# First mixer of a two-layer decoder trunk: GpSimd's wide elementwise work moved to VectorE

## The chip, the cores and the metric

The kernel runs on one core of a Trainium2 chip. The metric is device time in microseconds, the median over several executions. One more execution was profiled; all rows below come from it. The engines are named as in the profile: PE is TensorE (PEld its weight loads), DVE is VectorE, ACT is ScalarE, POOL is GpSimd, SP is SyncE, which issues the loads.

## What is computed

A trunk of two layers over 256 tokens of width 1024, in float32. Each layer has a token mixer (HGRN2, a gated linear recurrence, in the first layer; native sparse attention in the second) and a gated ConvFFN. Each of these is preceded by an RMS norm whose output is scaled and shifted by rows of a modulation that come from a conditioning vector `c`. The part of the reference that the change touches:

```
c_act = jax.nn.silu(c)
for layer in range(DEPTH):
    mod = c_act @ ada_w[layer] + ada_b[layer]
    sh1, sc1, g1, sh2, sc2, g2 = [m[:, None, :] for m in jnp.split(mod, 6, axis=-1)]
    hmix = rmsnorm(x, norm_mix[layer]) * (1.0 + sc1) + sh1
    ...
    x = x + g1 * y
...
proj = h @ w_in                                   # HGRN2: queries, gates f, values i, output gates g
log_f = jnp.log(lb + (1.0 - lb) * jax.nn.sigmoid(f_pre))
k = (1.0 - lb) * jax.nn.sigmoid(-f_pre)
...
    b = jnp.cumsum(lfc, axis=2)
    o_inter = jnp.einsum('bhtk,bhkv->bhtv', qc * jnp.exp(b), state)
    scores = jnp.einsum('bhtk,bhsk,bhtsk->bhts', qc, kc, decay)
    o_intra = jnp.einsum('bhts,bhsv->bhtv', scores, vc)
```

## The kernel before

Activations are feature-major: eight chunks of 128 features by 256 tokens. Every float32 product is made of three: the operands are split into a high and a low part (`hi`, `lo`), and the products high-high, high-low and low-high are added up in PSUM (`mm3`, L315).

**The stream of weights.** All weights pass in units of 128 x 1024 (512 KB), in the order of their use (`Stream`, L68). SP loads a unit into one of seven buffers `raw` (L93); a load starts when an earlier unit's buffer comes free. A unit of a weight is split: ScalarE rounds it to `whi` (L106) and another engine subtracts, `wlo = raw - whi` (L113). Five pairs of split parts exist. A unit of the modulation (`ada`) has one row of its weight per partition; its product with `silu(c)`, held on all partitions in `cb`, is summed along the columns into one column of `mod`. VectorE does that in one instruction with a sum (L244). GpSimd does the product alone (L241), and ScalarE then copies it with a sum (L242). Sixteen rows belong to the opening, 24 to the rest of the mixer, where they stand among the weights.

**The opening** (to about 75 us, L471). Instructions of VectorE, ScalarE and GpSimd go out here in the order of the code. One step per chunk: a row of the modulation, the chunk's scale and shift (`gs_t`, `sh_t`), the normed chunk `xn`, its high part `XH` on ScalarE and its low part `XL` on VectorE, and the split of the chunk's two units of weights. TensorE multiplies each chunk as soon as it is there. GpSimd has the second row of each of seven steps, and in chunks 2 to 5 (`U1`) half of the second low part.

**The recurrence** (class `HG`, L539, for four heads at a time, group A and then group B). `prepare` makes queries `Q`, decays `T` and keys `KS` out of PSUM, where GpSimd scales the keys (L575). Then `chain`: the scores of the diagonal (L585), five levels (m = 1 to 16; `level`, L592, scores L599) and three larger blocks (`blocks`, L622, scores L630, L641, L648). After each, `grow` multiplies half of the queries `QP` (VectorE, L617) and half of the keys (GpSimd, L618) by `T`, in two instructions of 256 columns each, and the next level's scores need both. Masked copies (L588, L605) take the scores out of PSUM on VectorE. `values` (L657) and `turn` (L689) make the outputs, which `finish_out` projects and adds to the residual (L448).

TensorE and SP follow the order of the code everywhere. While group A's chain runs, TensorE has the products for the queries and gates of group B beside it; beside group B's chain it has those of the output gates. Outside the opening a scheduler orders VectorE, ScalarE and GpSimd by priority; what the chain needs has `soon()`, and splits and rows fill in.

Of the six units ahead of the mixer's later rows GpSimd makes three low parts whole (`HG_LOW`), and of the 24 later rows it has every second one (`HG_POOL`).

Of the kernel before, what the change touches and what calls it, by code (L numbers as in the profile page):

```python
# [21 lines left out]
NC = 8            # feature chunks of D  # L22
S = 256
EPS = 1e-6
H = 8             # HGRN2 heads
LEVELS = (1, 2, 4, 8, 16)
G = 4             # NSA key/value groups
# [3 lines left out]
NJ = 22           # chunks of the ConvFFN's width  # L31
NJ0 = 4           # of them, those of a ConvFFN's first products
BIG = 3.0e38
# Order of issue. Units are 1024 columns of a weight, priorities are instructions.
RAWS, SPLITS = 7, 5           # buffers of loaded and of split units
LOOK = (7, 3)                 # units loaded and split ahead of the one in use
SOON = 90                     # priority of what the tensor engine waits for
QSOON = (150, 150, 25, 25)    # the same for a group's queries
TSOON = 75                    # and for probabilities turned
U1 = range(2, 6)              # opening chunks whose second low part DVE and Pool share  # L40
HG_LATE = 6                   # units ahead of the first units of the modulation, in HGRN2
FFN_LATE = 8                  # and in a ConvFFN
HG_POOL = 2                   # every how many of the former go to Pool
HG_LOW = (0, 1, 2)            # units whose low part goes to Pool
NSA_LOW = (6, 8)
NSA_LOW2 = (0, 2, 5)
NSA_ROWS = (11, 3)            # units of the modulation among the keys' and values', and behind them
NSA_SPLIT = 2                 # units split between the values' products
PRE = 2                       # units loaded ahead across a norm
HG_WEAVE = (16.4, 15.5)       # times of the second chain of HGRN2 and of the products beside it  # L50
HG_TURN = 14                  # of these, steps ahead of the first heads' turn
HG_OUT = (1, 3)               # heads projected in the chain, and up to the second heads' turn
# [15 lines left out]


class Stream:  # L70
    """Weights in the order of their use, in units of 1024 columns: loads run ahead of the splits into two
    float32r parts, and the splits ahead of the products."""

    def __init__(self, nc, raw_pool, split_pool, look_load, look_split):
# [1174 lines left out]
```

## Time and profile before

| | |
|---|---|
| device time, median of 3 runs | 777.64 us (776.15 to 781.36) |
| span of the profiled execution | 774.9 us |
| busy in it: PE, DVE, ACT, POOL | 725.1, 598.5, 410.4, 230.6 us |
| instructions of POOL | 247 |

The profile gives the span of its own execution, first to last instruction; what a run's time has beyond that it does not list. Busy time is the time in which an engine has an instruction open, whether it moves or not. In a timeline row stand the start and the length in us, then engine, line, operation, output<-inputs, size, and in brackets the idle time ahead of it and what ended that. In a row of a group stand its count and busy time, the mean of one in ns, and the idle time ahead.

### The profile page before, as it was taken

The numbers are of one execution on the slowest core, as the hardware profiler recorded it, in microseconds if no ns is written. First come the engines' busy times: TensorE is split into PE (matmuls) and PEld (weight loads), VectorE is DVE, ScalarE is ACT, GpSimd is POOL, SyncE is SP. The second block draws the span as 40 slices with busy tenths as digits, with TensorE's granted clock in tenths as the row PEclk, the third lists the DMA queues.
The fourth block names the chain that finished last, engine by engine and source line by source line (L and its number), as shares of the span: only waits on it lengthen the run. The fifth ranks groups of instructions, "written<-read, shape, count | busy, mean of one in ns | idle before, by whom it ended". The sixth has DMA issues, their size and how long they took to land.

```text
span 774.9 us, 14443 instructions
## 1 busy us (share of the span) xinstructions
PE 725.1 (94%) x5492; PEld 678.1 (88%) x5492; DVE 598.5 (77%) x1041; ACT 410.4 (53%) x756; POOL 230.6 (30%) x247
## 2 busy tenths in 40 slices
PE   7879888888999999999999999999999999999996
PEld 6767778768999999999989987756889999999995
DVE  5999987898599788778969877886768866666653
ACT  4456325426366444446545676776545744555544
POOL 4455647564203135111130015543520201101102
PEclk8999989999999999999999999987999999999998
DMA  8789655755368888899957960010237666776701
GB/s 302 269 274 313 204 191 191 268 192 193 110 219 300 297 280 270 294 267 341 344 191 254 355 207 21 35 56 1 85 134 271 196 217 214 215 221 210 209 18 55
DMA packets 48855, 160.45 MB, mean 207 GB/s; under 512 B 9362, under 2 KB 9618, under 8 KB 48787
## 3 DMA queue, kind: packets, MB, share of 16 engines
q1 hardware_dynamic: 48496, 159.02, 61.8%
q8 instruction: 43, 0.70, 0.4%
q10 hardware_dynamic: 290, 0.53, 0.2%
q14 instruction: 26, 0.20, 0.1%
HBM read 158.48 MB, written 1.05 MB: 206 GB/s over the span
## 4 chain that ended last, share of the span: by engine, by line
PE 72%; DVE 14%; issue 5%; POOL 5%; ACT 3%; DMA 2%; POOLq 0%; DVEq 0%; ACTq 0%
PE mm L316 10%; PE mm L318 10%; PE mm L317 10%; PE acc L379 9%; PE acc L317 7%; PE acc L316 7%; PE acc L318 7%; DVE wlo L113 4%; DVE raw L244 4%; PE acc L1006 2%; PE aux L1076 2%; PE aux L599 2%; POOL wlo L113 1%; PE acc L1005 1%; DMA raw<-ada 1%
## 5 line engine op out<-in xcount | busy, mean ns | idle before, releaser
L113 DVE TENSOR_TENSOR wlo<-raw,whi 128x1024 fp32r<-128x1024 f32 x193 | 247.1, 1291 | 66.8 <-ACT whi L106 66.5
L106 ACT CAST whi<-raw 128x1024 fp32r<-128x1024 f32 x201 | 207.9, 1047 | 138.2 <-PE acc L317 56.3
L316 PE MATMUL mm<-XH,whi 128*128 128x256 f32 x640 | 180.8, 283 | 1.0 <-DVE ff L791 0.9
L318 PE MATMUL mm<-XH,wlo 128*128 128x256 f32 x640 | 178.7, 279 | 0.0
L317 PE MATMUL mm<-XL,whi 128*128 128x256 f32 x640 | 178.4, 279 | 0.0
L796 POOL TENSOR_TENSOR fl<-ff,fh 128x256 fp32r<-128x256 f32 x44 | 43.9, 1002 | 302.9 <-ACT fh L794 297.8
L244 DVE SCALAR_TENSOR_TENSOR raw<-raw,cb 128x1024 f32<-128x1024 f32 x77 | 107.1, 1392 | 25.3 <-DMA raw<-ada 25.2
L316 PEld LDWEIGHTS mm<-XH,whi 128*128 128x128 f32 x640 | 119.9, 187 | 3.9 <-DVE ff L791 1.4
L318 PEld LDWEIGHTS mm<-XH,wlo 128*128 128x128 f32 x640 | 120.2, 188 | 0.0
L317 PEld LDWEIGHTS mm<-XL,whi 128*128 128x128 f32 x640 | 120.1, 188 | 0.0
L317 PE MATMUL acc<-fl,whi 128*128 128x256 f32 x352 | 98.5, 280 | 0.3 <-POOL fl L796 0.3
L316 PE MATMUL acc<-fh,whi 128*128 128x256 f32 x352 | 98.5, 280 | 0.0
L318 PE MATMUL acc<-fh,wlo 128*128 128x256 f32 x352 | 98.4, 280 | 0.0
L317 PEld LDWEIGHTS acc<-fl,whi 128*128 128x128 f32 x352 | 66.2, 188 | 0.5 <-POOL fl L796 0.5
L318 PEld LDWEIGHTS acc<-fh,wlo 128*128 128x128 f32 x352 | 66.2, 188 | 0.0
L316 PEld LDWEIGHTS acc<-fh,whi 128*128 128x128 f32 x352 | 66.1, 188 | 0.0
L241 POOL TENSOR_TENSOR raw<-raw,cb 128x1024 f32<-128x1024 f32 x19 | 49.4, 2599 | 14.2 <-DVE sh_t L414 9.2
L113 POOL TENSOR_TENSOR wlo<-raw,whi 128x1024 fp32r<-128x1024 f32 (+1 forms) x12 | 30.7, 2558 | 69.4 <-ACT whi L106 69.4
L379 PE MATMUL acc<-XH,whi 128*128 128x256 f32 x256 | 36.2, 283 | 8.8 <-ACT XH L398 8.0
L789 ACT ACTIVATE cv<-cv 128x256 f32<-128x256 f32 x44 | 18.0, 415 | 46.8 <-DVE cv L788 46.5
L379 PEld LDWEIGHTS acc<-XH,whi 128*128 128x128 f32 x256 | 32.5, 188 | 11.6 <-ACT XH L398 10.3
L1028 POOL TENSOR_SCALAR PR<-PR,rsum 128x128 f32<-128x128 f32 (+1 forms) x64 | 28.3, 463 | 43.3 <-DVE SC L1015 24.0
(221 smaller groups left out, 1456.4 us busy)
## 6 DMA issues: line engine op xcount, KB each, us to landing
raw<-ada SPq DMA_DIRECT2D x96, 512.0 KB, 4.9
raw<-up SPq DMA_DIRECT2D x88, 512.0 KB, 4.6
raw<-down SPq DMA_DIRECT2D x44, 512.0 KB, 4.5
raw<-hg_a SPq DMA_DIRECT2D x16, 512.0 KB, 5.9
raw<-hg_b SPq DMA_DIRECT2D x8, 512.0 KB, 5.8
raw<-hg_out SPq DMA_DIRECT2D x8, 512.0 KB, 4.5
raw<-nsa_a SPq DMA_DIRECT2D x8, 512.0 KB, 4.8
raw<-nsa_q SPq DMA_DIRECT2D x8, 512.0 KB, 4.9
```

Of the source, the lines that this page charges most:

```text
L106: self.nc.scalar.copy(hi, t)
L113: eng.tensor_sub(lo[:, c], t[:, c], hi[:, c].bitcast(FT))
L241: nc.gpsimd.tensor_mul(t, t, cb)
L244: nc.vector.scalar_tensor_tensor(t, t, 1.0, cb, op0=OP.mult, op1=OP.mult, accum_out=m)
L316: nc.tensor.matmul(o, wh, xh, start=start, stop=False, skip_group_check=True)
L317: nc.tensor.matmul(o, wh, xl, start=False, stop=False, skip_group_check=True)
L318: nc.tensor.matmul(o, wl, xh, start=False, stop=stop, skip_group_check=True)
L379: nc.tensor.matmul(half(accs, m), a[:, w], x[:, c], start=c == 0 and m % 2 == 0 and n == 0, stop=c == NC - 1 and n == 2, skip_group_check= ...
L599: nc.tensor.matmul(ps[:, (2 * h + t) * 64:(2 * h + t + 1) * 64], self.KS[:, h, x], q, start=True, stop=True)
L789: nc.scalar.activation(t, t, AF.Silu)
L796: return nc.gpsimd.tensor_sub(fl, f, fh.bitcast(FT))
L1028: nc.gpsimd.tensor_scalar(p, p, r[:, t, br:br + 1], 0.0, op0=OP.mult, op1=OP.add)
```

## The change

All of this work in the first layer's mixer goes to VectorE: the 7 + 12 modulation rows become VectorE's one instruction with a sum (so that ScalarE's 19 copies fall away), the three whole and four half low parts are made by VectorE (a low part is one instruction again), and VectorE scales the keys and multiplies them in `grow`. GpSimd keeps its small work and what it has in the other layers. The rest of the diff removes comments; line numbers of the changed file are smaller by 7 to 12 (L113 is L106 there, L244 L232, L399 L387, L574 to L576 L562 to L564, L588 L576, L605 L593, L617 and L618 L605 and L606, L620 L608, L681 L669, L742 L730).

```diff
-U1 = range(2, 6)              # opening chunks whose second low part DVE and Pool share
...
-HG_POOL = 2                   # every how many of the former go to Pool
-HG_LOW = (0, 1, 2)            # units whose low part goes to Pool
...
         def rest():
-            parts = low if isinstance(low, tuple) else (low,)
-            w = D // len(parts)
-            for n, eng in enumerate(parts):
-                c = slice(n * w, (n + 1) * w)
-                eng.tensor_sub(lo[:, c], t[:, c], hi[:, c].bitcast(FT))
+            low.tensor_sub(lo, t, hi.bitcast(FT))
...
-    def ada(n, pool=False):
-        """One row of the modulation's weights per partition, times silu(c), summed."""
+    def ada(n):
+
         def then(t):
-            m = mod[:, n:n + 1]
-            if pool:
-                nc.gpsimd.tensor_mul(t, t, cb)
-                return lambda: nc.scalar.activation(t, t, AF.Copy, accum_out=m)
-            else:
-                nc.vector.scalar_tensor_tensor(t, t, 1.0, cb, op0=OP.mult, op1=OP.mult, accum_out=m)
+            nc.vector.scalar_tensor_tensor(t, t, 1.0, cb, op0=OP.mult, op1=OP.mult, accum_out=mod[:, n:n + 1])
         return st.add(I["ada"][:, n], then)
 
...
-            ada(2 * c + 2, pool=True)
-        u_a[c].append(st.add(I["hg_a"][:, c, 1], low=(nc.vector, nc.gpsimd) if c in U1 else None))
+            ada(2 * c + 2)
+        u_a[c].append(st.add(I["hg_a"][:, c, 1]))
     ws = pairs(I["hg_i2"]) + chunks(I["hg_b"]) + pairs(I["hg_g2"]) + chunks(I["hg_out"])
-    ids = mix(ws[:HG_LATE], [], low=HG_LOW) + mix(ws[HG_LATE:], ada_units(0, "g1") + ada_units(0, "2"), range(0, 24, HG_POOL))
+    ids = mix(ws[:HG_LATE], []) + mix(ws[HG_LATE:], ada_units(0, "g1") + ada_units(0, "2"))
...
-                nc.gpsimd.tensor_scalar(self.KS[:, h], self.KS[:, h], a, 0.0, op0=OP.mult, op1=OP.add)
+                nc.vector.tensor_scalar(self.KS[:, h], self.KS[:, h], a, None, op0=OP.mult)
...
-                    nc.gpsimd.tensor_mul(k[:, hs], k[:, hs], T[:, hs, :, 1:2].to_broadcast([P, 2, n // 2, m]))
+                    nc.vector.tensor_mul(k[:, hs], k[:, hs], T[:, hs, :, 1:2].to_broadcast([P, 2, n // 2, m]))
```

TensorE and SP have the same order in both. The **first place** is VectorE's queue in the opening, from one `XL` to the next (`xn` and `XL` make one chunk of the normed residual). It stood as follows, here with a halved low part:

```order
L399 SCALAR_TENSOR_TENSOR XL<-xn,sh_t,XH 128x256
L113 TENSOR_TENSOR wlo<-raw,whi 128x1024
L113 TENSOR_TENSOR wlo<-raw,whi 128x512
L244 SCALAR_TENSOR_TENSOR raw,mod<-raw,cb 128x1024
L407 SCALAR_TENSOR_TENSOR gs_t<-mod,adab_94,small 128x1
L414 TENSOR_TENSOR sh_t<-mod,small 128x1
L397 SCALAR_TENSOR_TENSOR xn<-XT,gs_t,Rs 128x256
L399 SCALAR_TENSOR_TENSOR XL<-xn,sh_t,XH 128x256
```

In the changed kernel VectorE's queue reads, from one `XL` to the next:

```order
L387 SCALAR_TENSOR_TENSOR XL<-xn,sh_t,XH 128x256
L106 TENSOR_TENSOR wlo<-raw,whi 128x1024
L232 SCALAR_TENSOR_TENSOR raw,mod<-raw,cb 128x1024
L106 TENSOR_TENSOR wlo<-raw,whi 128x1024
L232 SCALAR_TENSOR_TENSOR raw,mod<-raw,cb 128x1024
L395 SCALAR_TENSOR_TENSOR gs_t<-mod,adab_94,small 128x1
L402 TENSOR_TENSOR sh_t<-mod,small 128x1
L385 SCALAR_TENSOR_TENSOR xn<-XT,gs_t,Rs 128x256
L387 SCALAR_TENSOR_TENSOR XL<-xn,sh_t,XH 128x256
```

The second low part is whole, and the step's second row of the modulation stands between the two.

The **second place** is VectorE's queue behind the opening, where it takes group A's queries out of PSUM (`hq`), makes decays (`ht`), and empties the two banks that TensorE needs next (the copies to `V`). Before:

```order
L113 TENSOR_TENSOR wlo<-raw,whi 128x1024 x2
L571 COPY hq<-acc 128x512 x2
L574 TENSOR_SCALAR ht<-hsg,lbt 128x256 x2
L742 COPY V_117<-mm 128x512
L574 TENSOR_SCALAR ht<-hsg,lbt 128x256 x2
L742 COPY V_118<-mm 128x512
L576 TENSOR_TENSOR hqp<-hq,ht 128x1024
L620 TENSOR_TENSOR ht_856<-ht 128x512
L620 TENSOR_TENSOR ht_898<-ht_856 128x4x64
L113 TENSOR_TENSOR wlo<-raw,whi 128x1024 x2
```

Behind these rows the masked copies of the diagonal (`hst`, L588) come at once. In the changed kernel the queue reads, from the product that makes `hqp` up to those masked copies:

```order
L564 TENSOR_TENSOR hqp<-hq,ht 128x1024
L106 TENSOR_TENSOR wlo<-raw,whi 128x1024 x2
L608 TENSOR_TENSOR ht_845<-ht 128x512
L730 COPY V_117<-mm 128x512
L730 COPY V_118<-mm 128x512
L106 TENSOR_TENSOR wlo<-raw,whi 128x1024
L608 TENSOR_TENSOR ht_886<-ht_845 128x4x64
L106 TENSOR_TENSOR wlo<-raw,whi 128x1024
L232 SCALAR_TENSOR_TENSOR raw,mod<-raw,cb 128x1024 x3
L106 TENSOR_TENSOR wlo<-raw,whi 128x1024
L232 SCALAR_TENSOR_TENSOR raw,mod<-raw,cb 128x1024
L576 COPY_PREDICATED hst<-masks,aux 128x2x128 x4
```

Ahead of these rows now stand one low part and the eight scalings of `ht` and `hks` in turn. The copies to `V` have moved behind three low parts and two products, and four rows of the modulation stand ahead of the masked copies.

The **third place** is VectorE's queue at the end of group B, from the outputs (`hO`) to the residual (`XT`), which it adds up when the last projection is there. Before:

```order
L325 TENSOR_SCALAR msq<-hss 128x8
L681 SCALAR_TENSOR_TENSOR hO<-aux,rst,SG_119 128x128 x4
L681 SCALAR_TENSOR_TENSOR hO<-aux,rst,SG_120 128x128 x4
L113 TENSOR_TENSOR wlo<-raw,whi 128x1024 x2
L701 SCALAR_TENSOR_TENSOR OL<-aux,small,OH 128x512 x2
L113 TENSOR_TENSOR wlo<-raw,whi 128x1024 x2
L448 SCALAR_TENSOR_TENSOR XT<-acc,gt_t,XT 128x256 x8
```

In the changed kernel the queue reads, at the same place:

```order
L669 SCALAR_TENSOR_TENSOR hO<-aux,rst,SG_119 128x128 x4
L669 SCALAR_TENSOR_TENSOR hO<-aux,rst,SG_120 128x128 x4
L232 SCALAR_TENSOR_TENSOR raw,mod<-raw,cb 128x1024
L689 SCALAR_TENSOR_TENSOR OL<-aux,small,OH 128x512 x2
L106 TENSOR_TENSOR wlo<-raw,whi 128x1024
L232 SCALAR_TENSOR_TENSOR raw,mod<-raw,cb 128x1024 x2
L106 TENSOR_TENSOR wlo<-raw,whi 128x1024
L232 SCALAR_TENSOR_TENSOR raw,mod<-raw,cb 128x1024
L106 TENSOR_TENSOR wlo<-raw,whi 128x1024
L232 SCALAR_TENSOR_TENSOR raw,mod<-raw,cb 128x1024
L436 SCALAR_TENSOR_TENSOR XT<-acc,gt_t,XT 128x256 x2
```

Five rows of the modulation (L232) now stand among the low parts of the output weights, where none stood. Ahead of this piece, behind the last product of the decays, stand four, where two stood, and one more (one before as well) is among the last products of the queries.

## Rows read from the trace of the kernel before

**Rows 1.** The profile's page, first line: the profiled execution's span.

```profile
span 774.9 us, 14443 instructions
```

**Rows 2.** Windows: span, busy us of PE, PEld, DVE, ACT, POOL, clock, DMA.

```profile
13.30:69.10 55.80, 46.94 (x279) 41.02 (x278) 50.39 (x63) 26.01 (x38) 25.25 (x11) 0.94 0.81 276
69.10:209.70 140.60, 121.83 (x899) 112.28 (x897) 117.63 (x170) 66.56 (x127) 78.23 (x58) 0.93 0.62 209
```

**Rows 3.** VectorE's groups, 10 to 210 us: line, operation, tiles, count | busy, mean ns.

```profile
L113 DVE TENSOR_TENSOR wlo<-raw,whi 128x1024 fp32r<-128x1024 f32 x35 | 47.3, 1366 | 9.2 <-ACT whi L106 9.2
L244 DVE SCALAR_TENSOR_TENSOR raw<-raw,cb 128x1024 f32<-128x1024 f32 x21 | 35.0, 1665 | 0.0
L617 DVE TENSOR_TENSOR hqp<-hqp,ht 128x256 f32<-128x256 f32 x28 | 25.8, 947 | 2.3 <-PE aux L599 1.9 <-PE aux L641 0.3
```

**Rows 4.** VectorE, least/median/greatest ns of three lines, 10 to 210 us.

```profile
L244 DVE SCALAR_TENSOR_TENSOR raw<-raw,cb x21: 1208/1218/3419, 10.8 to 186.0; 128x1024 f32<-128x1024 f32 x21
...
L113 DVE TENSOR_TENSOR wlo<-raw,whi x39: 679/1218/3137, 18.6 to 201.1; 128x1024 fp32r<-128x1024 f32 x35, 128x512 fp32r<-128x512 f32 x4
...
L617 DVE TENSOR_TENSOR hqp<-hqp,ht x28: 404/436/2596, 92.1 to 180.4; 128x256 f32<-128x256 f32 x28
```

**Rows 5.** GpSimd's two largest groups, 10 to 210 us, columns as in group 3.

```profile
L241 POOL TENSOR_TENSOR raw<-raw,cb 128x1024 f32<-128x1024 f32 x19 | 49.4, 2599 | 14.2 <-DVE sh_t L414 9.2 <-DMA raw<-ada 3.0 <-DVE wlo L113 1.9
L618 POOL TENSOR_TENSOR hks<-hks,ht 128x256 f32<-128x256 f32 x28 | 26.8, 970 | 35.5 <-PE aux L599 25.8 <-issue 5.2 <-DVE OL L701 1.8
```

**Rows 6.** Timeline, start and length in us: GpSimd, then VectorE, in the opening.

```profile
50.55 2.84 POOL L241 TENSOR_TENSOR raw<-raw,cb 128x1024 f32<-128x1024 f32 x1
...
51.06 3.41 DVE L244 SCALAR_TENSOR_TENSOR raw<-raw,cb 128x1024 f32<-128x1024 f32 x1
```

**Rows 7.** VectorE's timeline: low part of the normed chunk, four of eight.

```profile
17.64 0.48 DVE L399 SCALAR_TENSOR_TENSOR XL<-xn,sh_t,XH 128x256 fp32r<-128x256 f32 x1 [0.58 <-ACT XH L398]
...
55.82 0.48 DVE L399 SCALAR_TENSOR_TENSOR XL<-xn,sh_t,XH 128x256 fp32r<-128x256 f32 x1 [0.57 <-ACT XH L398]
...
63.82 0.48 DVE L399 SCALAR_TENSOR_TENSOR XL<-xn,sh_t,XH 128x256 fp32r<-128x256 f32 x1 [0.57 <-ACT XH L398]
...
69.08 0.48 DVE L399 SCALAR_TENSOR_TENSOR XL<-xn,sh_t,XH 128x256 fp32r<-128x256 f32 x1 [0.58 <-ACT XH L398]
```

**Rows 8.** TensorE's timeline: first product, first weights, and the scores of the levels.

```profile
75.54 0.47 PE L316 MATMUL mm<-whi,XH 128*128 128x512 f32 x1 [0.17 <-DVE V L742]
...
87.20 0.39 PE L318 MATMUL acc<-XH,wlo 128*128 128x256 f32 x1 [3.16 <-DVE wlo L113]
...
90.97 2.00 PE L599 MATMUL aux<-hqp,hks 128*128 128x64 f32 x16
...
108.12 3.53 PE L599 MATMUL aux<-hqp,hks 128*128 128x64 f32 x16 [2.31 <-DVE hqp L617]
...
119.61 0.70 PE L630 MATMUL aux<-hqp,hks 128*32 128x32 f32 x32
...
151.02 1.89 PE L599 MATMUL aux<-hqp,hks 128*128 128x64 f32 x16
...
166.54 1.89 PE L599 MATMUL aux<-hqp,hks 128*128 128x64 f32 x16
...
169.72 1.96 PE L599 MATMUL aux<-hqp,hks 128*128 128x64 f32 x16
...
176.29 0.94 PE L630 MATMUL aux<-hqp,hks 128*32 128x32 f32 x32 [2.97 <-DVE ht L620]
```

**Rows 9.** GpSimd and VectorE between the two chains.

```profile
122.67 4.91 POOL L618 TENSOR_TENSOR hks<-hks,ht 128x256 f32<-128x256 f32 x2 [0.90 <-PE aux L641]
...
138.73 3.29 DVE L576 TENSOR_TENSOR hqp<-hq,ht 128x1024 f32<-128x1024 f32 x1
```

**Rows 10.** Granted clock (PEclk) of one stretch, columns as in group 2.

```profile
108.00:115.00 7.00, 6.88 (x33) 6.91 (x34) 4.76 (x6) 1.10 (x3) 3.85 (x3) 0.52 0.49 163
```

**Rows 11.** Loads of weights, 60 to 210 us, from issue to landing.

```profile
DMA to landing us min/median/max: 3.4/4.5/7.0
```

More of the change, by code (lines that the diff above doesn't have):

```diff
@@ L251, in ada_units, with mix @@
         return list(range(b + a, b + e))
-    def mix(ws, adas_, pool=(), low=()):
+    def mix(ws, adas_, low=()):
         ids, n, m = [], len(ws), len(adas_)
@@ L259, in mix @@
             while done < m and done * n < (k + 1) * m:
-                ada(adas_[done], done in pool)
+                ada(adas_[done])
                 done += 1
```

## The prediction, made before the changed kernel ran

> **What bounds the kernel now.** I read the page first, for the span [rows 1], then the windows of the two stretches that the change touches: the opening (13.3 to 69.1 us) and the rest of the HGRN2 mixer (69.1 to 209.7 us) [rows 2]. Over their 196.4 us TensorE is busy 46.9 + 121.8 = 168.8 us and VectorE 50.4 + 117.6 = 168.0 us: two engines at 86% that wait for each other, and a clock of 0.93 to 0.94 says that TensorE is at times at the lower of its two levels. GpSimd is busy 25.3 + 78.2 = 103.5 us. Everything behind 209.7 us is untouched by the change (the order of instructions there is the same on every engine), so I carry it over.
>
> Then VectorE's groups against their own least and median durations [rows 3, 4]. A 1024-column modulation row has a median of 1.22 us but a mean of 1.67 and a greatest of 3.42; a key-side neighbour, the query product L617, has a least of 0.40 us, a mean of 0.95 and a greatest of 2.60. The timeline shows why: GpSimd's row starts at 50.55 and ends at 53.39, VectorE's row starts at 51.06 and lasts to 54.47, which is GpSimd's end plus 1.08 [rows 6]. While GpSimd works on such a tile, VectorE's instruction of two SBUF inputs stands still, and GpSimd's own rows are stretched in turn.
>
> The Trainium skill, "SBUF — State Buffer", section "SBUF: two separate sides", says that a VectorE instruction with two SBUF inputs and a GpSimd instruction that reads SBUF hold one shared pair of ports in turn, as a lock for the whole instruction. The rows above agree with it.
>
> **The change, part by part.** VectorE gains 19 modulation rows (7 in the opening, 12 later), 19 x 1.22 = 23.2 us; three whole low parts and four halves, 3 x 1.22 + 4 x (1.22 - 0.68) = 5.8; 28 key products of the size of L617, 28 x 0.40 = 11.3; eight key scalings of 256 columns, for which no VectorE row exists, and which I price like L617's least, 8 x 0.40 = 3.2 (bounds 0 and, at L617's mean, 7.6) [rows 4]. Together 43.5 us. GpSimd loses its two largest groups, 49.4 and 26.8 us [rows 5], and more.
>
> What VectorE gets back is its blocked time, mean less median (or least) times count [rows 3, 4]: low parts 35 x 0.15 = 5.2, rows 21 x 0.45 = 9.4, query products 28 x 0.54 = 15.2, and 2.1 from one 1024-column product that took 3.29 us [rows 9]. That is 32 us, the smaller groups not counted. So VectorE's busy time in the stretch becomes about 168 + 43.5 - 32 = 180 of 196 us: about level. The gain or loss lies in what TensorE waits for, stage by stage.
>
> *Opening.* VectorE's queue sets the step: between the normed low parts at 55.82 and 63.82 lie 8.0 us, of which one row and half a low part are blocked by GpSimd; between those at 63.82 and 69.08, with GpSimd idle, 5.26 [rows 7]. The changed queue's step (the first place shown in the section on the change) is this work, two whole low parts and one row, plus one more row, so 5.26 + 1.22 = 6.5. From 17.64 to 69.08 there are seven steps, 51.4 us; seven of 6.5 are 45.5: **-6**. What could stop it is the loads, four units of 0.5 MB in each 6.5 us; landing takes 4.5 us in the median and 7.0 at most [rows 11], and seven buffers at 1.6 us a unit give 11, so I charge nothing.
>
> *First preparation.* TensorE's token-major products need the banks that the copies to V empty, and start at 75.54 as soon as they do [rows 8]. These copies now stand behind a low part, eight scalings, a 1024-column product, two low parts and a product of 512 columns (half of 1.22): 1.22 + 3.2 + 1.22 + 2.44 + 0.6 = 8.7 us, instead of two scalings. TensorE starts about 6.5 later. It had waited 3.16 us at 87.20 for the first weights, which are now split in time, and the masked copies behind the products give way too, so level 0 (now at 90.97) comes **+2**.
>
> *Levels, heads 0 to 3.* From 90.97 to 119.61 five levels take 28.6 us, 5.7 each [rows 8]. After: the scores 1.8 (the 2.00 of the row less overlap), two masked copies and four products of 256 columns on VectorE, six of 0.40: 4.2, in which TensorE's other products fit. Five times 1.5: **-7.6**. Low parts and rows run in VectorE's wait for the scores.
>
> *Between the chains.* From 119.61 to 151.02 stand two key products that took GpSimd 4.91 us instead of 2 x 0.40 and a 3.29 us query product [rows 9]: 4.1 + 2.1, of which TensorE feels nearly all: **-5**.
>
> *Levels, heads 4 to 7.* 151.02 to 176.29, 25.3 us; five of 4.2 are 21: **-4.3**.
>
> *Tail, 176.29 to 209.7.* The last growths carry four more products, +1.6. Ten modulation rows instead of three now stand on VectorE between the last level and the last low part of the output weights (the third place shown); seven more are 8.5 us. The bounds are nothing (VectorE is idle for 140.6 - 117.6 = 23 us of this stretch [rows 2], mostly here) and 8.5; the low parts are due one after the other and the rows lie between them, so I take about a third, 3.0: together **+4.6**.
>
> The sum is -6 + 2 - 7.6 - 5 - 4.3 + 4.6 = -16.3. I take back 5 for the clock: behind the 2.31 us wait at 108.12 the same scores took 3.53 instead of 2.00 us, and 108 to 115 us ran at a granted clock of 0.52 [rows 8, 10], 1.2 instead of 2.4 GHz, which costs up to 3.5 us; the new waits at the first preparation and in the tail are longer than that one, and may bring one such stretch each, 2 x 2.5. Forecast **-11.3**. The profiled span is 774.9; the runs shown have a median of 777.64, 2.7 above it, so I set 777.6 - 11.3 = **766.3 us**. Removed GpSimd and ScalarE work (19 sums) I price at nothing: both have room beside it, and the weights' casts on ScalarE only come earlier.
>
> **Rivals.** *No change to speak of.* VectorE's queue is in order, and at the second place shown three rows and one more stand ahead of the masked copies of the diagonal; their loads start when buffers come free a few instructions earlier on the same queue. At 4.5 us a load each waits under 1 us, at 7.0 about 2 to 3, for three rows up to 7; the chain then starts 6 later and the gain is 5: 772. For it: the queue was filled by priority and not by the loads' real length. Against: in the stretch now VectorE hardly ever waits for a load.
>
> *Slower: the key products were hidden.* On GpSimd they can run beside VectorE's masked copies. Where no modulation row is in the way a level takes 169.72 - 166.54 = 3.2 us [rows 8]; in line on VectorE it takes 4.2. If 3.2 were the rule, ten levels would cost +10, with preparation and tail +6.6, opening -6: 788. It decides once levels come out above about 5.3. Against: the ten now average 5.4.
>
> *Slower: VectorE is the bound by its busy time.* If 168.0 us were work and not blocking, 211.5 us would not fit in 196.4: +15, 793. Against: the medians [rows 4]. The Trainium skill, "Perfetto Trace Analysis", section "Identifying the Most-Contended Engine", would have the fullest engine relieved first, which speaks against this change; its section "Optimizing Scalar/DVE Operations" adds that shifting between VectorE and GpSimd may not help.
>
> *More.* No clock loss, loads in time: -16 to -20, 757.5 to 761.
>
> **How the numbers follow.** Forecast (-8 to -15) 0.55, more 0.08, about no change 0.22, hidden keys 0.10, VectorE the bound 0.05. A measurement of this kernel tells about 1%, 7.8 us, from no change. Faster by more: 0.55 + 0.08, less the 0.03 of the forecast that ends short: 0.60; slower 0.14 (the two rivals but for their mild ends); same 0.26. The range goes from 757 (no allowance, every load in time) to 778 (the tail's rows unhidden, +5.5, and loads at 7.0, +6): 8 in 10. The likeliest case alone spans 762 to 770.
>
> **What would show it.** Right: rows on VectorE with a mean near 1.25 instead of 1.67; opening steps of 6.5; levels of 4.2; GpSimd nearly empty to 200 us; TensorE idle at the V copies for about 6 us. Wrong: VectorE waiting for row loads ahead of the masked copies, levels above 5, or an end of the mixer later than 205 us. The largest risk is the tail, where a planner's order and not a sum decides what TensorE waits for.

## The result, and the profile after

The changed kernel takes 759.02 us in the median (756.25 to 761.95), the kernel before 777.61 beside it: a ratio of 0.9752, 95% interval 0.9718 to 0.9786, faster by about 19 us. The forecast was 766.3 with a range of 757 to 778. The page of the changed kernel, span and first table:

```profile
span 755.6 us, 14337 instructions
PE 719.0 (95%) x5492; PEld 672.2 (89%) x5492; DVE 588.7 (78%) x1118; ACT 390.8 (52%) x718; POOL 133.0 (18%) x185
```

The span of the profiled execution is 19.3 us shorter [rows 1]. Where the 19.3 lie is read from the marks that the prediction used: in the changed kernel the first and the last normed low part of the opening (VectorE), TensorE's first product behind the copies to `V`, the first scores of the levels, the scores of the 32-blocks, both again for heads 4 to 7, and the last chunk of the residual (VectorE); the last line is that chunk in the kernel before.

```profile
16.59 0.48 DVE L387 SCALAR_TENSOR_TENSOR XL<-xn,sh_t,XH 128x256 fp32r<-128x256 f32 x1 [0.57 <-ACT XH L386]
61.93 0.49 DVE L387 SCALAR_TENSOR_TENSOR XL<-xn,sh_t,XH 128x256 fp32r<-128x256 f32 x1 [0.58 <-ACT XH L386]
74.12 0.77 PE L304 MATMUL mm<-whi,XH 128*128 128x512 f32 x1 [6.27 <-DVE V L730]
86.51 1.97 PE L587 MATMUL aux<-hqp,hks 128*128 128x64 f32 x16
107.75 0.70 PE L618 MATMUL aux<-hqp,hks 128*32 128x32 f32 x32
131.58 1.89 PE L587 MATMUL aux<-hqp,hks 128*128 128x64 f32 x16
153.06 0.70 PE L618 MATMUL aux<-hqp,hks 128*32 128x32 f32 x32 [2.55 <-DVE OL L689]
188.15 0.48 DVE L436 SCALAR_TENSOR_TENSOR XT<-acc,gt_t,XT 128x256 f32<-128x256 f32 x1 [0.57 <-PE acc L306]
```
```profile
208.73 0.48 DVE L448 SCALAR_TENSOR_TENSOR XT<-acc,gt_t,XT 128x256 f32<-128x256 f32 x1 [0.60 <-PE acc L318]
```

Set against [rows 7, 8] the differences between neighbouring marks are:

| stretch | before, us | after, us | measured | forecast |
|---|---|---|---|---|
| start to the first normed low part | 17.64 | 16.59 | -1.1 | not priced |
| opening, seven steps | 51.44 | 45.34 | -6.1 | -6 |
| first preparation, to level 0 | 21.89 | 24.58 | +2.7 | +2 |
| levels, heads 0 to 3 | 28.64 | 21.24 | -7.4 | -7.6 |
| between the chains | 31.41 | 23.83 | -7.6 | -5 |
| levels, heads 4 to 7 | 25.27 | 21.48 | -3.8 | -4.3 |
| tail, to the last residual chunk | 32.44 | 35.09 | +2.7 | +4.6 |
| all behind | 566.2 | 567.5 | +1.3 | 0 |
| allowance for the clock | | | | +5 |
| together | 774.9 | 755.6 | -19.3 | -11.3 |

The windows of the six stretches from 13.3 us on (columns as in [rows 2]), first of the kernel before, then of the changed one:

```profile
13.30:69.08 55.78, 46.92 (x279) 41.02 (x278) 50.37 (x63) 25.99 (x38) 25.25 (x11) 0.94 0.81 275
69.08:90.97 21.89, 18.17 (x100) 15.55 (x99) 21.56 (x22) 14.48 (x18) 13.53 (x8) 0.93 0.74 259
90.97:119.61 28.64, 24.44 (x180) 23.86 (x180) 24.78 (x34) 9.94 (x14) 16.95 (x14) 0.88 0.59 201
119.61:151.02 31.41, 25.97 (x202) 23.42 (x202) 24.35 (x43) 16.11 (x41) 20.53 (x13) 0.95 0.65 218
151.02:176.29 25.27, 19.86 (x123) 17.07 (x122) 23.11 (x34) 7.86 (x11) 15.34 (x13) 0.93 0.61 207
176.29:208.73 32.44, 32.44 (x288) 31.42 (x289) 23.37 (x39) 17.80 (x43) 11.88 (x11) 0.95 0.55 179
```
```profile
13.30:61.93 48.63, 46.12 (x282) 40.38 (x280) 42.90 (x76) 18.89 (x24) 0.00 (x0) 0.95 0.93 320
61.93:86.51 24.58, 18.29 (x98) 15.67 (x98) 21.97 (x35) 13.43 (x16) 0.00 (x0) 0.86 0.86 298
86.51:107.75 21.24, 20.90 (x180) 20.60 (x179) 19.00 (x43) 6.59 (x8) 0.00 (x0) 1.00 0.59 184
107.75:131.58 23.83, 23.83 (x202) 21.72 (x202) 22.20 (x52) 11.31 (x32) 1.75 (x1) 1.00 0.53 163
131.58:153.06 21.48, 18.12 (x123) 15.74 (x122) 19.93 (x47) 4.41 (x5) 0.00 (x0) 1.00 0.53 164
153.06:188.15 35.09, 33.09 (x288) 31.41 (x289) 32.51 (x62) 17.83 (x42) 7.15 (x6) 0.95 0.84 293
```

Two things are to be seen. In the opening VectorE has 76 instructions instead of 63 and is busy for 42.9 instead of 50.4 us: more work, less time. And from 86.51 to 131.58 TensorE is busy for 44.7 of 45.1 us at a granted clock of 1.00. VectorE's groups of the changed kernel, 10 to 192 us, answer to [rows 3, 4]:

```profile
L106 DVE TENSOR_TENSOR wlo<-raw,whi 128x1024 fp32r<-128x1024 f32 x42 | 51.1, 1220 | 0.5 <-ACT whi L103 0.5
L232 DVE SCALAR_TENSOR_TENSOR raw<-raw,cb 128x1024 f32<-128x1024 f32 x40 | 48.6, 1220 | 2.6 <-DMA raw<-ada 2.6
L605 DVE TENSOR_TENSOR hqp<-hqp,ht 128x256 f32<-128x256 f32 x28 | 11.8, 423 | 0.0
L606 DVE TENSOR_TENSOR hks<-hks,ht 128x256 f32<-128x256 f32 x28 | 11.8, 420 | 0.0
```

Every mean is now close to the median of before: 1.22 (mean before 1.67) us for a row, 0.42 (before 0.95, median 0.44) for a query product.

### The profile page after: what moved, and what is told of

The parts are those of the page before. It is cut to its first block, busy times and chain, and to the rows that moved or that the text cites. A ratio compares the mean times of both kernels' runs of the same rounds, so it can differ in the third digit from the quotient of the medians.

```text
span 755.6 us, 14337 instructions
## 1 busy us (share of the span) xinstructions
PE 719.0 (95%) x5492; PEld 672.2 (89%) x5492; DVE 588.7 (78%) x1118; ACT 390.8 (52%) x718; POOL 133.0 (18%) x185
## 3 DMA queue, kind: packets, MB, share of 16 engines
HBM read 158.48 MB, written 1.05 MB: 211 GB/s over the span
## 4 chain that ended last, share of the span: by engine, by line
PE 75%; DVE 13%; issue 4%; POOL 3%; ACT 2%; DMA 1%; POOLq 0%; DVEq 0%; ACTq 0%
PE mm L304 11%; PE mm L306 11%; PE mm L305 11%; PE acc L367 9%; PE acc L304 7%; PE acc L305 6%; PE acc L306 6%; DVE wlo L106 4%; DVE raw L232 4%; PE aux L587 2%; PE acc L994 2%; PE aux L1064 2%; POOL sq L340 2%; PE acc L993 1%; PE aux L890 1%
## 5 line engine op out<-in xcount | busy, mean ns | idle before, releaser
L106 DVE TENSOR_TENSOR wlo<-raw,whi 128x1024 fp32r<-128x1024 f32 x196 | 243.6, 1249 | 60.5 <-ACT whi L103 60.2
L232 DVE SCALAR_TENSOR_TENSOR raw<-raw,cb 128x1024 f32<-128x1024 f32 x96 | 123.3, 1288 | 26.0 <-DMA raw<-ada 25.8
L784 POOL TENSOR_TENSOR fl<-ff,fh 128x256 fp32r<-128x256 f32 x44 | 41.8, 953 | 304.6 <-ACT fh L782 297.2
L367 PEld LDWEIGHTS acc<-XH,whi 128*128 128x128 f32 x256 | 32.4, 188 | 7.6 <-ACT XH L386 7.5
L314 POOL TENSOR_TENSOR rst<-msq,mhalf 128x2 f32<-128x2 f32 (+1 forms) x7 | 8.7, 1237 | 166.7 <-DVE msq L313 166.7
L386 ACT ACTIVATE XH<-xn,sh_t 128x256 fp32r<-128x256 f32 x32 | 15.3, 503 | 41.9 <-DVE xn L385 41.9
```

The costliest lines, as they stand in the source:

```text
L106: low.tensor_sub(lo, t, hi.bitcast(FT))
L232: nc.vector.scalar_tensor_tensor(t, t, 1.0, cb, op0=OP.mult, op1=OP.mult, accum_out=mod[:, n:n + 1])
L367: nc.tensor.matmul(half(accs, m), a[:, w], x[:, c], start=c == 0 and m % 2 == 0 and n == 0, stop=c == NC - 1 and n == 2, skip_group_check= ...
L386: hi = nc.scalar.activation(XH[:, c], xn, AF.Identity, bias=sh)
L784: return nc.gpsimd.tensor_sub(fl, f, fh.bitcast(FT))
```

## The experiments

The theory is that GpSimd's wide tiles hold VectorE's up, so that their time counts on VectorE's queue. The rivals are that the gain comes from work that is simply finished sooner (the key products, the sums on ScalarE, the buffers of the loads), or that VectorE's long instructions are its own work. Beside the ratio to the kernel before, each run is judged by the start of the last residual chunk (208.73 before, 188.15 after). What follows that chunk takes 564 to 576 us in the profiled executions of the kernels here, of which only two have an edit there (five low parts in the run with one input, the low parts `fl` in the last run), so the chunk tells more of the mixer than the whole time does. Each start is read from one profiled execution; the last run, which has no edit ahead of it, has 188.24 where the changed kernel has 188.15.

### The opening alone

```
-            ada(2 * c + 2, pool=True)
+            ada(2 * c + 2)
-        u_a[c].append(st.add(I["hg_a"][:, c, 1], low=(nc.vector, nc.gpsimd) if c in U1 else None))
+        u_a[c].append(st.add(I["hg_a"][:, c, 1], low=None))
```

> Only the opening is changed: its seven GpSimd rows and four halved low parts go to VectorE; all of GpSimd's work behind the opening stays. If GpSimd's tiles of two inputs are what stretches VectorE's, the steps come down from 7.35 to about 6.4 us as in the changed kernel, the last normed low part comes near 62 instead of 69 us, and since nothing behind is touched the whole time falls by about 7 us: 770.5 (768 to 773). If VectorE's long instructions in the opening are its own work, it gains 10.7 us of it and the time rises to 780 or more.

Ratio 0.9891 (0.9839 to 0.9942), which is -8.5 us; the medians, 772.45 and 778.51, lie 6.1 apart. VectorE's last normed low part of the opening, and TensorE's first product behind the copies to `V`:

```profile
62.26 0.48 DVE L399 SCALAR_TENSOR_TENSOR XL<-xn,sh_t,XH 128x256 fp32r<-128x256 f32 x1 [0.58 <-ACT XH L398]
70.55 0.77 PE L316 MATMUL mm<-whi,XH 128*128 128x512 f32 x1 [2.49 <-DVE V L742]
```

The steps are 6.47 us (16.95 to 62.26). More work on VectorE made its queue shorter, which excludes the rival that its long instructions are its own work. The last residual chunk is at 204.09, 4.6 earlier: 2.2 of the 6.8 us were lost again in the mixer.

### The keys alone

```
-                nc.gpsimd.tensor_scalar(self.KS[:, h], self.KS[:, h], a, 0.0, op0=OP.mult, op1=OP.add)
+                nc.vector.tensor_scalar(self.KS[:, h], self.KS[:, h], a, None, op0=OP.mult)
...
-                    nc.gpsimd.tensor_mul(k[:, hs], k[:, hs], T[:, hs, :, 1:2].to_broadcast([P, 2, n // 2, m]))
+                    nc.vector.tensor_mul(k[:, hs], k[:, hs], T[:, hs, :, 1:2].to_broadcast([P, 2, n // 2, m]))
```

> Only the key scalings and key products go to VectorE; GpSimd keeps all rows and low parts. If GpSimd's work blocks VectorE, the rows that are left (five or so in each chain) go on blocking, so only a part of the levels' gain comes: levels of about 4.8 us instead of 5.4, and 3 us between the chains, against 2 us in the preparation, where the copies to V move back: about -7, 770 (765 to 775). If the key products were hidden beside the masked copies, the levels get longer by 0.8 and the time is 780 to 788. If the key products alone made the levels slow, all of the gain of the chains comes here: 762 or less.

Ratio 0.9979 (0.9935 to 1.0024): no change, where 7 us were expected. TensorE behind the copies to `V`, and VectorE's row and query product (10 to 205 us):

```profile
85.44 0.76 PE L316 MATMUL mm<-whi,XH 128*128 128x512 f32 x1 [9.65 <-DVE V L742]
98.08 1.89 PE L599 MATMUL aux<-hqp,hks 128*128 128x64 f32 x16
```
```profile
L244 DVE SCALAR_TENSOR_TENSOR raw<-raw,cb 128x1024 f32<-128x1024 f32 x21 | 36.0, 1719 | 0.0
L617 DVE TENSOR_TENSOR hqp<-hqp,ht 128x256 f32<-128x256 f32 x28 | 16.6, 594 | 1.5 <-PE aux L599 1.5
```

The levels came to 4.7 us as expected (98.08 to 121.44), but the preparation took 28.6 instead of 21.9, since the copies to `V` now stand behind the scalings and the product for the queries while GpSimd's low parts and rows go on holding VectorE up. The row's mean did not move (1.72).

### All but the key products

Against the changed kernel:

```
-                    nc.vector.tensor_mul(k[:, hs], k[:, hs], T[:, hs, :, 1:2].to_broadcast([P, 2, n // 2, m]))
+                    nc.gpsimd.tensor_mul(k[:, hs], k[:, hs], T[:, hs, :, 1:2].to_broadcast([P, 2, n // 2, m]))
```

> All of the change but the 28 key products, which stay on GpSimd; no other large GpSimd work stands beside the chains. If the two key products of a level and the two query products shut each other out, a level takes the scores' 1.9 plus about 2.6 us of products, 4.5, and the time is near the changed kernel's: 757 to 763. If key products beside masked copies are really hidden, levels go to 3.2 us and the time to about 750. If the levels were slow because GpSimd makes the key products late by itself, they stay at 5.4 and the time is 768 or more.

Ratio 0.9754 (0.9701 to 0.9806): all of the gain, with the key products where they were. Levels of heads 0 to 3 take 4.3 us (85.68 to 107.27). Among its waits of TensorE (us in total, times, longest) the key products still stand behind the levels, ahead of the scores of the 128-blocks (113.71 and 115.27), and not in them:

```profile
PE aux L648 <- POOL hks L618: 2.6, 2, 1.8
```

The expected reason, four products in turn, is not what sets 4.3 us. In the changed kernel TensorE's timeline between two levels reads:

```profile
88.28 0.36 PE L304 MATMUL acc<-XH,whi 128*128 128x256 f32 x1
...
90.64 0.28 PE L306 MATMUL acc<-XH,wlo 128*128 128x256 f32 x1
91.25 1.97 PE L587 MATMUL aux<-hqp,hks 128*128 128x64 f32 x16 [0.34 <-DVE hks L606]
```

From 88.28 to 90.64 it issues 21 products of group B's queries without a gap, about 0.12 us apart, 2.5 us; with the 1.8 from the scores' start to the first of them a level takes TensorE itself about 4.25. This one took 4.74 with its wait; the five average 4.25 (21.24 / 5), of which TensorE is busy for 20.90 of the 21.24 us. It is so here too, and nearly so (4.1) in the run with one input below. The arithmetic on VectorE, 4.2, agreed with it by chance.

### One input instead of two on GpSimd

```
-                nc.gpsimd.tensor_mul(t, t, cb)
+                nc.gpsimd.tensor_scalar(t, t, 1.0, 0.0, op0=OP.mult, op1=OP.add)
...
-                eng.tensor_sub(lo[:, c], t[:, c], hi[:, c].bitcast(FT))
+                (eng.tensor_scalar(lo[:, c], t[:, c], 1.0, 0.0, op0=OP.mult, op1=OP.add) if eng is self.nc.gpsimd
+                 else eng.tensor_sub(lo[:, c], t[:, c], hi[:, c].bitcast(FT)))
...
-                    nc.gpsimd.tensor_mul(k[:, hs], k[:, hs], T[:, hs, :, 1:2].to_broadcast([P, 2, n // 2, m]))
+                    nc.gpsimd.tensor_scalar(k[:, hs], k[:, hs], 1.0, 0.0, op0=OP.mult, op1=OP.add)
```

> The kernel before with the same order on TensorE, VectorE, ScalarE and SyncE; GpSimd's rows, low parts and key products keep their places and output sizes, but each reads one tile (times 1.0) instead of two, so that the modulation, some weights' low parts and the growth of the keys are left out of the computation. If it is a tile of two inputs on GpSimd that stops a VectorE instruction of two inputs, VectorE's rows come to a mean of about 1.25 instead of 1.67 us, its query products to 0.45 instead of 0.95, and the time falls by 8 to 15 us (763 to 770), as long as GpSimd's own instructions get no longer. If GpSimd merely being busy, or being slow, is what costs, VectorE's means and the time stay as they were, 775 to 780.

Ratio 0.9493 (0.9449 to 0.9538), 741.35 us, far more than expected; the last residual chunk comes at 172.80, 35.9 earlier. GpSimd's row and VectorE's row, query product (10 to 175 us), and one meeting of the two engines:

```profile
L241 POOL TENSOR_SCALAR raw<-raw 128x1024 f32<-128x1024 f32 x19 | 23.8, 1255 | 28.0 <-DMA raw<-ada 19.1 <-DVE wlo L113 8.9
```
```profile
L244 DVE SCALAR_TENSOR_TENSOR raw<-raw,cb 128x1024 f32<-128x1024 f32 x21 | 27.4, 1305 | 0.0
L617 DVE TENSOR_TENSOR hqp<-hqp,ht 128x256 f32<-128x256 f32 x28 | 15.6, 587 | 0.5 <-PE aux L599 0.3 <-PE aux L630 0.2
```
```profile
25.82 1.24 POOL L241 TENSOR_SCALAR raw<-raw 128x1024 f32<-128x1024 f32 x1 [6.00 <-DVE wlo L113]
```
```profile
26.05 2.06 DVE L244 SCALAR_TENSOR_TENSOR raw<-raw,cb 128x1024 f32<-128x1024 f32 x1
```

The number of GpSimd's inputs is not what decides: a tile of one input ends at 27.06, and VectorE's row that started beside it ends at 28.11, 1.05 later. What changed is how long GpSimd's tile lasts: 1.26 us in the mean instead of 2.60 [rows 5]. Its rows, key products and low parts together fell from 92.0 to 52.7 us, 39.3 less, and the mixer ended 35.9 earlier, with VectorE's work and every order on the other engines untouched. ScalarE's 19 sums stay too (it is busy for 410.5 us, 410.4 before), so the gain does not need them gone. The run also ends each row sooner, and with one input a low part no longer waits for `whi` nor a key product for `ht`, so that alone it does not exclude the rival of work finished sooner; for that stands the next one. Shorter tiles on GpSimd brought more (35.9 us) than moving them (20.6), but this kernel leaves part of the computation out.

### GpSimd loaded again, with work that nobody waits for

Against the changed kernel; `more` holds for the 19 rows that the change moved:

```
             nc.vector.scalar_tensor_tensor(t, t, 1.0, cb, op0=OP.mult, op1=OP.mult, accum_out=mod[:, n:n + 1])
+            if more:
+                nc.gpsimd.tensor_copy(junk[0][:, :1], mod[:, n:n + 1])
+                nc.gpsimd.tensor_mul(junk[0], junk[0], cb)
...
```

> The changed kernel with its own work untouched and GpSimd loaded again: behind each of the 19 moved rows (still made by VectorE) GpSimd multiplies a tile of its own, 128x1024 with two inputs, whose result nobody reads; no weight buffer, no ScalarE sum and no wait of TensorE hangs on it, but for the two small steps of the norms (L314) that may queue behind one. If what GpSimd cost was that its tiles hold VectorE's up, 19 x 2.4 = 46 us of such tiles bring VectorE's rows back to a mean above 1.5 us and cost 10 to 30 us: 770 to 790. If the gain of the change came from rows, sums and buffers that are done sooner, these tiles cost nothing, or at most the 2 to 4 us of the norms: 757 to 764.

793.26 us, above the 790 that was expected at most, a ratio of 1.011 (1.0035 to 1.0185) to the kernel before: the whole gain is gone and more; the last residual chunk comes at 221.71 instead of 188.15. GpSimd's groups and one of VectorE's (10 to 220 us), and one meeting, GpSimd then VectorE:

```profile
L235 POOL TENSOR_TENSOR junk<-junk,cb 128x1024 f32<-128x1024 f32 x19 | 55.7, 2930 | 1.4
L234 POOL COPY junk<-mod 128x1 f32<-128x1 f32 x19 | 15.7, 827 | 124.4 <-DVE raw L232 123.1 <-DVE msq L318 1.2
```
```profile
L400 DVE SCALAR_TENSOR_TENSOR gs_t<-mod,adab,small 128x1 f32<-128x1 f32 x8 | 15.7, 1960 | 0.3
```
```profile
28.31 3.27 POOL L235 TENSOR_TENSOR junk<-junk,cb 128x1024 f32<-128x1024 f32 x1
```
```profile
29.37 2.23 DVE L400 SCALAR_TENSOR_TENSOR gs_t<-mod,adab,small 128x1 f32<-128x1 f32 x1
```

No result, sum or buffer hangs on these tiles, and 55.7 us of them, with 15.7 of the copies of one column that tie each to its row, cost 33.6. Nor is it GpSimd's own steps queued behind them: VectorE waits 3.2 us for the small steps of the norms, 3.1 in the changed kernel. The mean of VectorE's rows rose less than expected (1.36, not 1.5): here it is the small scale of the chunk, one column wide, that stands still until GpSimd's tile ends (31.60 and 31.58), 1.96 us in the mean where the changed kernel's mean is 0.22. That wait lies on the path of every step of the opening (8.5 us a step). This shows the holding up as a cause by itself. How much of the 19 us it makes the run does not give, since these tiles start right behind a row of VectorE and so stand at other places than GpSimd's work did.

### Rows and low parts only

The two edits of the opening alone, and:

```
-    ids = mix(ws[:HG_LATE], [], low=HG_LOW) + mix(ws[HG_LATE:], ada_units(0, "g1") + ada_units(0, "2"), range(0, 24, HG_POOL))
+    ids = mix(ws[:HG_LATE], []) + mix(ws[HG_LATE:], ada_units(0, "g1") + ada_units(0, "2"), ())
```

> Only rows and low parts go to VectorE (opening and mixer); key products and key scalings stay on GpSimd. Against the run that left only the key products on GpSimd (760.5) this differs by the eight key scalings. If these cost the preparation its time on VectorE, the copies to V come earlier, TensorE's wait for them falls from 6.3 to 4 us or less and the time to 755 to 758. If the scalings' engine makes no difference, because GpSimd's scalings hold VectorE up as long as VectorE's own take, it is 759 to 762.

Ratio 0.9667 (0.9569 to 0.9766). Its times lie between 751.38 and 766.86 us, too far apart to tell it from the changed kernel or to decide between the two cases expected. The last residual chunk comes at 185.10, 3.1 before the changed kernel's and 4.8 before that of all but the key products (189.92), which differs by the eight scalings alone. TensorE's first product behind the copies to `V`:

```profile
73.44 0.76 PE L316 MATMUL mm<-whi,XH 128*128 128x512 f32 x1 [5.93 <-DVE V L742]
```

The wait stays at 5.9 us where 4 or less was expected if the scalings made it: the copies stand behind low parts that the scheduler put first, whichever engine scales. Against the changed kernel the stretch between the chains is longer here (27.2 instead of 23.8 us; the weight load of the last scores waits 1.73 us for keys), the levels of heads 4 to 7 are shorter (18.9 instead of 21.5) and so is the tail (32.6 instead of 35.1). So in these two profiles what the keys gain in one place on VectorE they give back in two others. The levels of heads 4 to 7 bear that out in every other run with the key products on GpSimd and the rows on VectorE (19.5 to 20.2 us); of the tail it is not shown, since that took 35.0 us where only the opening was changed and 32.4 before.

### The copies to V moved ahead

Against the changed kernel:

```
-    for t in range(2):
-        nc.vector.tensor_copy(V[t][:, :512], ips[t])
     A = HG(0, acc)
     with soon():
+        for t in range(2):
+            nc.vector.tensor_copy(V[t][:, :512], ips[t])
         A.prepare()
```

> The changed kernel with one thing moved: the copies to V come ahead of the first preparation's decays and scalings and have the same priority as they. If the long wait of TensorE (6.27 us) is a matter of VectorE's order, it falls to about 2 us, the stretch of half clock behind it is gone, and the time falls by 4 to 6: 754 (752 to 757). If what TensorE gains there it waits for again at the first scores, because the scalings and the product for the queries come 1.3 us later, it stays at 757 to 760.

Ratio 0.9712 (0.9654 to 0.9769), not to be told from the changed kernel. TensorE's product, and a wait that is new:

```profile
68.27 0.47 PE L304 MATMUL mm<-whi,XH 128*128 128x512 f32 x1 [0.17 <-DVE V L732]
```
```profile
PE acc L306 <- DVE wlo L106: 5.8, 5, 1.8
```

The wait of 6.27 us is gone, and level 0 starts at 80.30 instead of 86.51. But the last residual chunk is at 187.01, 1.1 earlier: most of the 6.2 us is paid back in waits for low parts, of which this row alone has 5.8 us where the changed kernel has 1.7. VectorE, not the place of two copies, is what the mixer waits for now.

With the eight key scalings back on GpSimd as well:

```
-                nc.vector.tensor_scalar(self.KS[:, h], self.KS[:, h], a, None, op0=OP.mult)
+                nc.gpsimd.tensor_scalar(self.KS[:, h], self.KS[:, h], a, 0.0, op0=OP.mult, op1=OP.add)
```

> As the kernel with the copies to V moved ahead, and the eight key scalings back on GpSimd. If a GpSimd instruction holds VectorE's for its own length even with one input, 0.55 us for each on GpSimd take the place of 0.35 on VectorE and nothing is gained: the same as with the copies alone, within 2 us. If GpSimd's scalings with one input run beside VectorE, 2.8 us of VectorE's queue go and the time is 2 to 3 us shorter than with the copies alone.

Ratio 0.9646 (0.9597 to 0.9695), last residual chunk at 184.81: 2.2 us earlier than with the copies alone, so taking 2.8 us off VectorE does show, though GpSimd's tile of one input can hold VectorE up. Its trace gives a reason for one group: GpSimd's four scalings (67.63 to 69.58) run mostly beside the two copies to `V`, which read PSUM and take 1.29 us together as with the copies alone. Whether that is all is not shown.

With A's turn in the chain's priority beside the copies:

```
...
-one_after_another(first_of(g2, HG_TURN), A.turn(), g2, *outs[:HG_OUT[0]])
+one_after_another(first_of(g2, HG_TURN), critical(A.turn()), g2, *outs[:HG_OUT[0]])
...
```

> As the kernel with the copies to V moved ahead, and group A's turn (its OL) given the same priority as the chain of group B, so that the two OL stand ahead of the low part and row that they stood behind. If the 2.55 us that TensorE waits ahead of the scores of the 32-blocks (153.06 in the changed kernel) are VectorE's order, they go and the time is about 2 us shorter than with the copies alone. If the bank they wait for comes free no earlier, or the growth of the last level is what comes late next, no difference over 1 us.

Ratio 0.9739 (0.9681 to 0.9797), last residual chunk at 189.68: 2.7 us later, a miss. The wait ahead of the 32-blocks fell from 2.55 to 1.13, and TensorE waited 6.9 instead of 5.8 us for low parts and 1.7 instead of 0.6 for `hO`.

### The best of these together

The run with rows and low parts only, and the copies to `V` moved ahead in it by the diff above:

> Rows and low parts on VectorE, key products and key scalings on GpSimd, and the copies to V moved ahead of the first preparation. If VectorE's queue is what the rest of the mixer now waits for, TensorE's wait of 5.9 us for V goes and, unlike where VectorE also has the keys, most of it is kept: the last residual chunk at about 181 instead of 185.1 us, time 747 to 752. If TensorE waits for low parts instead, as it did where VectorE had the keys, only 1 us is left: residual at 184, time as with rows alone.

753.37 us, a ratio of 0.9626 (0.9576 to 0.9675). That is below the changed kernel's interval, though the kernel before was measured anew for it (783.04 us); beside the same measurement the last run, which is the changed kernel but for `fl`, has 0.9723. Level 0 comes 4.0 us earlier than without the copies moved (81.64 instead of 85.67), the last residual chunk only 0.3 (184.78): the second case of the expectation. With the two copies on ScalarE:

```
-            nc.vector.tensor_copy(V[t][:, :512], ips[t])
+            nc.scalar.copy(V[t][:, :512], ips[t])
```

> As the kernel before this one, but the two copies to V are made by ScalarE, which takes 1.3 us from VectorE and puts them ahead of ScalarE's sigmoids. If VectorE is the bound, 1 us shorter than with the copies on VectorE; if ScalarE's sigmoids, 1.3 us later, hold up the keys and decays, 1 to 2 us longer.

Ratio 0.9643 (0.959 to 0.9696), the last residual chunk 1.2 us earlier (183.59), which the whole time does not resolve.

### The same kind of work where TensorE is full

```
-            return nc.gpsimd.tensor_sub(fl, f, fh.bitcast(FT))
+            return nc.vector.tensor_sub(fl, f, fh.bitcast(FT))
```

> The changed kernel with GpSimd's largest work behind the first mixer, the low parts fl of the ConvFFN (44 of 0.95 us), on VectorE as well. TensorE is busy for 89 of 90 us there, so whatever VectorE gets back, nothing waits for it: the same as the changed kernel, 757 to 761. If GpSimd's hold on VectorE costs time wherever it stands, 5 us or more are gained.

Ratio 0.9723 (0.9666 to 0.9781), the same as the changed kernel, as expected. On VectorE one of these takes 0.42 us (0.95 on GpSimd):

```profile
L784 DVE TENSOR_TENSOR fl<-ff,fh x44: 411/421/428, 222.9 to 744.6; 128x256 fp32r<-128x256 f32 x44
```

## Why the prediction was right, and where it was not

**The sign and the mechanism** held. GpSimd's tiles stop VectorE's, shown by the run that loads GpSimd again. VectorE took on 43.6 us (19 rows of 1.22, 28 key products of 0.42, eight scalings of 0.35, 5.8 of low parts) and is busy for 158.5 us in the six windows, 9.0 less than before. The forecast was 180. By the lengths of its instructions it got back about 47 us where the prediction counted 32 and said that smaller groups were left out: these were worth about 14 (the products of the decays 5.6, half low parts 3.3, the small scales 2.0, the rest below 2 each). What is left of the difference is in the measure: neighbours overlap (two low parts of 1.22 take 2.35 us at 62.33), and busy time counts that once. The rival of the busy time fell with it.

**The stages** came out within 1 us in four of the six that were priced: the opening (steps of 6.48, forecast 6.5), the first preparation (TensorE starts 12.2 us behind the last normed low part instead of 6.5, so 5.7 later, forecast about 6.5; its wait is 6.27), and both sets of levels. For heads 4 to 7 that is luck in part: four levels take 3.5 to 4.0 us each, and the fifth 6.1, of which TensorE waits 2.55 behind `OL`.

**The step that failed is the clock**: "I take back 5 for the clock". The new stretches at half clock are there. TensorE's windows of the changed kernel behind the wait for `V` and behind the wait ahead of the 32-blocks:

```profile
74.00:77.00 3.00, 2.88 (x7) 2.33 (x8) 3.00 (x4) 0.00 (x0) 0.00 (x0) 0.50 0.82 269
...
155.00:160.00 5.00, 5.00 (x36) 4.60 (x35) 5.00 (x12) 4.07 (x7) 0.00 (x0) 0.70 0.46 127
```

With the copies to `V` moved ahead, that wait is gone and the clock from 62 to 80 us is 1.00. But both stages came out with them at +2.7 and +2.7, near or under what they were priced at without. And the prediction took only the new waits into account, not the old ones that go: where a wait went, so did the slow stretch behind it. In the six windows the length times one less the clock sums to 13.3 us before and 7.6 after: up by 1.9 in the first preparation, down elsewhere, 5.7 less together. This is read from the windows, which count idle time too, and no run tests it by itself. The stretch at 0.52 that the prediction itself showed [rows 10] lies where the changed kernel has 1.00. Without that allowance the sum was -16.3, within 3 of the -19.3 measured. So the measured time is that of the rival called "more", which had 0.08 and named just this condition; the likeliest case's own range, 762 to 770, missed it.

**Two terms were mis-sized.** Between the chains -5 was -7.6: TensorE has no gap left there, and its clock went from 0.95 to 1.00. The tail's +4.6 was +2.7; how that parts into products and rows is not shown, since the tails of runs with the same instructions there lie 2.6 us apart (32.4 and 35.0). The bound was misread too: of VectorE's 23 us without work only 9.1 lay in the tail, not most of them.

**One term was right for a wrong reason.** The levels' 4.2 us were worked out as VectorE's queue; for heads 0 to 3 it is TensorE's own work between two scores. The prediction laid much of the gain in the chains to the key products. The runs show that rows and low parts carry it: keys alone brought nothing, all but the key products brought everything, and rows with low parts alone reached the last residual chunk earlier than the whole change. The key products did shorten the stretch between the chains, as the prediction had it (23.8 us against 27.2 to 28.5 in the four runs with rows on VectorE and keys on GpSimd), though not where the copies to `V` were moved as well (26.1 to 28.6), and they lengthened the levels of heads 4 to 7; there the rival "the key products were hidden" had a point (3.2 us between some scores with the keys on GpSimd, as in [rows 8]), but TensorE's own 4.25 in heads 0 to 3 left it no room to decide.

**The rival of rows that wait for loads** was half there: VectorE waited 0.73 and 1.88 us for loads ahead of the masked copies of the diagonal, and no wait of TensorE followed, since it had products of group B to do.

## What to carry to other kernels

Where GpSimd and VectorE both read SBUF, count GpSimd's wide tiles as time on VectorE's queue: where the two meet, a tile that lasts 2.4 us there and 1.2 on VectorE is cheaper moved, however full VectorE looks, and the sign to look for is a VectorE group whose mean lies well above its median. Move what lasts longest first and only where TensorE waits; once TensorE or VectorE's own work bounds the stretch, the rest of the move brings nothing. When waits are added and removed, weigh the clock on both sides.

## What the runs showed of the hardware that was not expected

A GpSimd tile 128x1024 of one input took 1.08 us in the median where one of two inputs took 2.43, and it stops VectorE's instruction of two inputs all the same. The Trainium skill, "GPSIMD Engine Reference", section "4.1 Engine selection", has GpSimd about twice as slow as VectorE for two inputs and at roughly line rate for one. The 2.43 against VectorE's 1.22 agrees; the key scalings, one input of 256 columns, took 0.50 on GpSimd and 0.35 on VectorE in the median.

How small VectorE's instruction is does not matter: 128x1 took 2.23 us instead of 0.22 behind a tile of two inputs. Nor does it need two tiles: in the run that loads GpSimd again a scaling of the decays, one tile and two columns, took 2.49 us instead of 0.41 (140.55, GpSimd's tile from 140.49 to 142.89). VectorE's instructions that read PSUM, the masked copies (0.568 and 0.564 us) and the copies of the queries (0.687 and 0.685), were the same without GpSimd's tiles and with the 55.7 us of them, also in the middle of one, as four masked copies in that run, GpSimd then VectorE:

```profile
97.68 3.26 POOL L235 TENSOR_TENSOR junk<-junk,cb 128x1024 f32<-128x1024 f32 x1
```
```profile
98.62 1.44 DVE L583 COPY_PREDICATED hst<-masks,aux 128x256 f32<-128x256 uint32 x4
```

The four took 1.44 us in the changed kernel too, without a tile beside them.
